# Gated DeltaNet on one core: q projected during the block inversion, q and v parked in SBUF, key norms by products, few subtractions on GpSimd

## The chip, the cores and the metric

The kernel runs on one core of a Trainium2 chip. It has a matrix engine (TensorE, PE in the profile), three engines for elementwise work (VectorE or DVE, ScalarE or ACT, GpSimd or POOL), a queue that issues most transfers (SyncE, SP), a working memory of 128 partitions (SBUF) and an accumulator memory of eight banks that TensorE writes (PSUM). The engines run side by side and wait for each other by semaphores; each takes its instructions in a fixed order. The metric is the device time of one execution in microseconds.

## The reference

A trunk of four layers on 256 frames of 1024 features, in float32. The mixers are gated DeltaNet (GDN, layers 0 and 3), mLSTM (layer 1) and differential attention (layer 2); each is followed by an MLP of width 4096, and each of these eight sub-layers is wrapped in RMS norms. Only GDN and the order of some accumulations change. GDN in short:

```python
proj = h @ w_in                                   # q, k, v, z, gates
qkv = silu(causal_conv(proj[..., :GDN_QKV], conv_w))   # 4 taps in time
q, k, v = l2_norm(q), l2_norm(k), v
kb = kc * bc[..., None]                           # beta * k
a_mat = where(strict, einsum('nbhid,nbhjd->nbhij', kb, kc) * decay, 0)
t_mat = a_mat + eye
sol = triangular_solve(t_mat, concat([vc * beta, kb * exp(gc)]))
attn = einsum('nbhid,nbhjd->nbhij', qc, kc) * decay
# over chunks: v_new = value - kcd @ S;  o = q_inter @ S + attn @ v_new
#              S = S * exp(g_last) + k_state^T @ v_new
return (rms_norm(o, norm_g) * silu(z)) @ w_out
```

## The kernel before

**Products in three parts.** Each weight piece of 128x1024 arrives by one DMA as `raw_*`. `load_w` (L141) copies it on ACT to a short format (`whi_*`, L160), and DVE, or GpSimd for the pieces listed in `pool`, subtracts that copy from the raw piece (`wlo_*`, L166). Activations are split likewise (`hThi`, `hTlo`; `aThi`, `aTlo`). A product is the sum of hi·hi, lo·hi and hi·lo, three matmuls for each step of the contraction. There are four `raw` buffers (NRAW) and eight each of hi and lo (NW); a ninth piece waits until TensorE has finished with one before.

**GDN, in the order of the program** (L943 to L1442). The chunks of the reference are taken as two blocks of 128 frames for each of eight heads; `hg` is a group of four heads, `t` a block of frames.

1. The keys are projected with frames on partitions (`k_block`, tile `gkt`), transposed (`k_channels`, tile `gp`) and convolved in time (`conv`: the first tap on ACT, L1032, three more on DVE, L1038, then silu, L1039). `gates` computes decay and beta in many small steps on DVE; TensorE needs their result `gv` (L1010) for the running sums `gc` (L1016).
2. `decays` broadcasts rows of sums (`gcb`) and makes `Eup` (ACT Abs L1074, then Exp L1079), of which GpSimd keeps the triangles (L1080, L1081).
3. `grams` makes k·k (`gG`). The squared norms of the keys are its diagonal, summed on DVE (L1096, `ssk`); with `c2` = beta over squared norm, `L` becomes the scaled strict triangle (L1105); its 32x32 diagonal blocks are copied to `Lc` by DVE (L1109).
4. `base_inverse` (L1113) inverts all 32x32 blocks at once on DVE: one transpose to `LT` (L1117), 31 steps of a product into `Xt` (L1127) and a subtraction from `Xb` (L1131), 118 small instructions, each step needing the one before, and two transposes to `Xc` and `Yc` (L1132, L1133). `Xb` starts from an identity loaded by DMA (L1353).
5. `levels` joins blocks to 64 and 128 on TensorE, each level with copies on ACT between (`Za`, `Zb`, `zs`, `Ya`, `Yb`, `Zc`, `Yc`, L1136 to L1179); `v_tokens` turns v and scales it with `c1` into `rhs`; `solve`, `state`, `update`, `attend`, `q_norm`, `inter` and `output` follow. `q_norm` gets the squared norms of q by products of squares with a column of ones (`square_sums`, L1056, tile `gss`).
6. The output projection (`finish_mixer`, `out_steps`, tile `acc_wo_g`).

**What sets TensorE's order.** In GDN its order is the program's (`manual`). The projections that nothing waits for yet are generators in the list `blocks`; `fill(us)` takes matmuls off the head of the list until their planned cost (columns / 2400 us for each) is used up, and `finish(key)` takes them until a block is done. The amounts are the table `FILL`, one row for layer 0 and one for layer 3. The other engines' order comes from a scheduler at build time, by program order and readiness; `tc.issue_after(ins)` queues an instruction behind `ins` on the same engine, and the list `hold` does so for the weight splits.

Before, the list holds k and v ahead of the inversion. The blocks of q and z (`conv_block(0, q)`, `z_block`) are appended behind it in the program, and the fill of 23.2 (layer 0) or 21.4 (layer 3) at F[7] comes before the first level. Outputs of the v blocks stay in the PSUM bank, two of them in accumulator banks (`core`), until their convolution reads them.

**MLP and output projections.** Where 512 columns accumulate in each of two halves (`down` L530, `out_steps` L353), a piece of two contraction steps is used in the order k, then half, then the three parts:

```python
for k in range(2):
    for n, hs in enumerate(HALVES):
        seq = [(aTs[j][a][:, 2*q+k, ...], wt(b, k)[:, hs]) for a, b in ((0, 0), (1, 0), (0, 1))]
```

The token projections (`tok_seq`, tiles `mmt`, `gz`, `gkt`) take hi·hi for two k, lo·hi for two k and hi·lo for two k, in one bank.

Of the kernel before, what the change touches and what calls it, by code (L numbers as in the profile page):

```python
# [66 lines left out]
def trunk_kernel(  # L67
# [403 lines left out]
    def mlp(li, hT, first, second):  # L471
# [58 lines left out]
        def down(t, j, q):  # L530
            if (j, q) not in w2t:
                r0 = j * 512 + q * 256
                w2t[j, q] = load_w(w2[r0 : r0 + 256, :].rearrange("(k p) c -> p k c", p=P), 2, D, f"w2_{li}_{j}_{q}")
# [3 lines left out]
            for k in range(2):
                for n, hs in enumerate(HALVES):
                    seq = [(aTs[j][a][:, 2 * q + k, t * P : (t + 1) * P], wt(b, k)[:, hs]) for a, b in ((0, 0), (1, 0), (0, 1))]
                    tail = 3 if t and 8 * (j - nb + 2) + 4 * q + 2 * k + n >= TAIL[0] else 0  # L540
                    run(accs[t][n], seq, start=(j, q, k) == (0, 0, 0), stop=(j, q, k) == (nb - 1, 1, 1), tail=tail)
# [401 lines left out]
    def gdn(li, j, hT, first, second):  # L943
# [83 lines left out]
        def conv(s, q, ps, dst):  # L1027

            y = cvt(f"cy_{li}_{s}{q}") if dst is None else dst
# [3 lines left out]
            for ct in range(2):  # L1033
                b = s * 8 + q * 2 + ct
                x = ps[:, ct * T : (ct + 1) * T]
                for d in (1, 2, 3):
# [1 line left out]
                    nc.vector.scalar_tensor_tensor(y[:, ct, d:], x[:, : T - d], cw[:, c : c + 1], y[:, ct, d:], op0=ALU.mult, op1=ALU.add)  # L1038
            nc.scalar.activation(y, y, AF.Silu)  # L1039
            if s == 0:  # L1040
                squares[q] = cvt(f"csq_{li}_{q}")
                nc.scalar.activation(squares[q], y, AF.Square)
            return y
# [22 lines left out]
        def decays(hg, pr):  # L1066
# [9 lines left out]
            if pr == 1:  # L1076
                for t in range(NT):
                    e = Eup[hg, t]
                    nc.scalar.activation(e, e, AF.Exp, scale=-1.0)  # L1079
# [4 lines left out]
        def grams(hg):

            cols = slice(4 * hg, 4 * hg + 4)
            G = {}
# [10 lines left out]
            nc.vector.tensor_scalar(th8(ssk)[:, :, cols], th8(ssk)[:, :, cols], EPS, None, op0=ALU.add)
            nc.vector.reciprocal(th8(rk2)[:, :, cols], th8(ssk)[:, :, cols])
            nc.vector.tensor_tensor(th8(c2)[:, :, cols], th8(rk2)[:, :, cols], th8(beta)[:, :, cols], op=ALU.mult)  # L1100
            for t in range(NT):
                for h in range(4):
# [2 lines left out]
                    nc.vector.scalar_tensor_tensor(lo, G[t][:, h * P : (h + 1) * P], c2[:, c : c + 1], lo, op0=ALU.mult, op1=ALU.mult)  # L1105
# [32 lines left out]
        def levels():  # L1138
# [9 lines left out]
            nc.scalar.activation(zs[Q[2]], zb[Q[2]], AF.Copy, scale=-1.0)  # L1148
            for b in range(NB):
                for hg in range(2):  # L1150
                    nc.scalar.activation(yts[hg][Q[b], :, Q[b]], Yc[Q[b], hg * 8 : hg * 8 + 8, :], AF.Copy)
# [351 lines left out]
```

## Time and profile before

| quantity | value |
|---|---|
| median of 3 runs | 1379.69 us (1378.94 to 1380.14) |
| the profiled execution | 1379.3 us |
| its span, first to last instruction | 1377.6 us |
| mean granted TensorE clock | 0.974 |
| TensorE matmul, busy | 1308.7 us (95%), 8010 instructions |
| VectorE, busy | 850.9 us (62%), 1493 instructions |
| ScalarE, busy | 725.0 us (53%), 1226 instructions |
| GpSimd, busy | 244.6 us (18%), 225 instructions |
| moved by DMA | 222.77 MB, mean 162 GB/s |

Times in the profile count from the span's start. Layer 0's GDN runs from there to about 204 us, layer 3's from about 1000 to 1187 us; between lie MLP, mLSTM, MLP, attention and MLP. An engine's busy time includes time in which an instruction that has been issued is held up, so a long duration of a small instruction can be a wait. Matmuls overlap; the step from one start to the next tells their rate. A row of a group reads: line, engine, operation, output<-inputs, shapes, count | busy us, mean ns | idle time before them and what ended it. A row of the wait list reads: who waited <- for what: total us, times, longest. A row of the timeline or the chain starts with its start and its length in us.

### The profile page before, as it was taken

To read this page: it belongs to the slowest core of one execution; us is meant where nothing else is said; L and a number is where in the kernel's file an instruction comes from. 1 tells how busy PE (TensorE), PEld (TensorE's weight loads), DVE (VectorE), ACT (ScalarE), POOL (GpSimd) and SP (SyncE) were. 2 spreads that over 40 slices of the span, in tenths; PEclk is the share of its full clock that TensorE was granted. 3 is DMA by queue.
4 is the path that set the end of the run, shared out by engine and by line. 5 is a ranking of instruction groups with operands and counts; after the bars stand their busy time and mean duration, and the time that the engine had idled before them with its cause. 6 is when DMAs were issued, how large, how long until landed. Compare 5 with 4: busy or idle time off the path is not lost.

```text
span 1377.6 us, 20856 instructions
## 1 busy us (share of the span) xinstructions
PE 1308.7 (95%) x8010; PEld 1135.3 (82%) x8010; DVE 850.9 (62%) x1493; ACT 725.0 (53%) x1226; POOL 244.6 (18%) x225
## 2 busy tenths in 40 slices
PE   8885999999999999999999999999999499999998
PEld 5784978898888888989877788989879488899996
DVE  5696577555575786555555477555577944865452
ACT  6754756444454555444465656444467285555441
POOL 2492340000010110000031110000047427000000
PEclk9897999999999999999998999999999799999999
DMA  7452148565655356665463147555554413566650
GB/s 255 130 164 82 47 139 259 184 183 184 201 179 173 99 183 213 191 185 190 138 212 123 62 156 241 184 184 185 185 165 118 123 63 123 167 203 190 183 190 33
DMA packets 131627, 222.77 MB, mean 162 GB/s; under 512 B 10883, under 2 KB 81093, under 8 KB 131526
## 3 DMA queue, kind: packets, MB, share of 16 engines
q1 hardware_dynamic: 131524, 221.42, 50.7%
q8 instruction: 63, 1.03, 0.3%
q14 instruction: 38, 0.31, 0.1%
q10 hardware_dynamic: 2, 0.00, 0.0%
HBM read 220.35 MB, written 1.05 MB: 161 GB/s over the span
## 4 chain that ended last, share of the span: by engine, by line
PE 81%; DVE 11%; ACT 3%; DMA 2%; issue 1%; POOL 1%; SPq 0%; DVEq 0%; POOLq 0%; ACTq 0%
PE acc_mlp L174 26%; PE mmc L174 20%; PE mmt L174 6%; PE acc_wo_g L174 3%; PE gz L174 3%; DVE Xb L1131 2%; DVE Xt L1127 2%; PE dq L174 2%; PE dv L174 2%; PE mo L174 2%; PE acc_wo_d L174 2%; PE acc_wo_m L174 2%; PE mqk L174 2%; PE gp L174 2%; PE acc_S L174 2%
## 5 line engine op out<-in xcount | busy, mean ns | idle before, releaser
L166 DVE TENSOR_TENSOR wlo_w<-raw_w,whi_w 128x1024 fp32r<-128x1024 f32 x256 | 307.2, 1223 | 217.4 <-ACT whi_w L160 216.8
L160 ACT ACTIVATE whi_w<-raw_w 128x1024 fp32r<-128x1024 f32 x256 | 264.3, 1056 | 220.2 <-PE mmc L174 103.3
L174 PE MATMUL acc_mlp<-whi_w,aThi 128*128 128x512 f32 x512 | 202.9, 396 | 0.0
L174 PE MATMUL acc_mlp<-whi_w,aTlo 128*128 128x512 f32 x512 | 202.5, 396 | 0.0
L174 PE MATMUL acc_mlp<-wlo_w,aThi 128*128 128x512 f32 x512 | 202.5, 395 | 0.0
L139 POOL TENSOR_TENSOR rr<-ms,mhalf 128x1 f32<-128x1 f32 x32 | 17.4, 544 | 604.7 <-DVE ms L251 604.7
L174 PEld LDWEIGHTS acc_mlp<-wlo_w,aThi 128*128 128x128 f32 x512 | 96.3, 188 | 23.3
L174 PEld LDWEIGHTS acc_mlp<-whi_w,aThi 128*128 128x128 f32 x512 | 96.4, 188 | 22.0
L174 PEld LDWEIGHTS acc_mlp<-whi_w,aTlo 128*128 128x128 f32 x512 | 96.3, 188 | 22.0
L174 PE MATMUL mmc<-hThi,wlo_w 128*128 128x256 f32 x768 | 108.7, 283 | 0.0
L174 PE MATMUL mmc<-hTlo,whi_w 128*128 128x256 f32 x768 | 107.8, 283 | 0.0
L174 PE MATMUL mmc<-hThi,whi_w 128*128 128x256 f32 x768 | 107.7, 283 | 0.0
L174 PEld LDWEIGHTS mmc<-hThi,whi_w 128*128 128x128 f32 x768 | 99.9, 191 | 1.8
L174 PEld LDWEIGHTS mmc<-hThi,wlo_w 128*128 128x128 f32 x768 | 99.3, 192 | 0.0
L174 PEld LDWEIGHTS mmc<-hTlo,whi_w 128*128 128x128 f32 x768 | 99.0, 192 | 0.0
L166 POOL TENSOR_TENSOR wlo_g<-raw_g,whi_g 128x1024 fp32r<-128x1024 f32 x32 | 76.0, 2406 | 33.5 <-ACT whi_g L160 29.1
L524 ACT ACTIVATE aThi<-rc 128x512 fp32r<-128x512 f32 x48 | 30.3, 632 | 77.8 <-DVE rc L522 77.8
L525 DVE TENSOR_TENSOR aTlo<-rc,aThi 128x512 fp32r<-128x512 f32 x48 | 33.2, 692 | 32.6 <-ACT aThi L524 32.6
L166 POOL TENSOR_TENSOR wlo_wo_g<-raw_wo_g,whi_wo_g 128x1024 fp32r<-128x1024 f32 x16 | 37.6, 2376 | 45.5 <-ACT whi_wo_g L160 44.5
L166 POOL TENSOR_TENSOR wlo_gz<-raw_gz,whi_gz 128x1024 fp32r<-128x1024 f32 x16 | 37.7, 2391 | 42.9 <-ACT whi_gz L160 42.9
L225 ACT ACTIVATE hThi<-T_pre 128x512 fp32r<-128x512 f32 x32 | 17.5, 595 | 49.9 <-PE T_pre L220 49.9
L160 ACT ACTIVATE whi_g<-raw_g 128x1024 fp32r<-128x1024 f32 x32 | 33.3, 1059 | 15.4 <-DMA raw_g<-in_gdn_w_in_dram 11.6
(418 smaller groups left out, 2566.5 us busy)
## 6 DMA issues: line engine op xcount, KB each, us to landing
raw_w<-in_mlp_w_dram SPq DMA_DIRECT2D x256, 512.0 KB, 4.2
raw_g<-in_gdn_w_in_dram SPq DMA_DIRECT2D x32, 512.0 KB, 3.8
raw_gk<-in_gdn_w_in_dram SPq DMA_DIRECT2D x16, 512.0 KB, 5.0
raw_gz<-in_gdn_w_in_dram SPq DMA_DIRECT2D x16, 512.0 KB, 3.6
raw_wo_g<-in_gdn_w_out_dram SPq DMA_DIRECT2D x16, 512.0 KB, 3.3
raw_d<-in_diff_w_in_dram SPq DMA_DIRECT2D x16, 512.0 KB, 4.4
gpost<-in_norm_g_dram SPq DMA_DIRECT2D x8, 512.0 KB, 4.8
raw_mv<-in_mlstm_w_in_dram SPq DMA_DIRECT2D x8, 512.0 KB, 4.5
```

What stands on the lines that cost most here:

```text
L139: return nc.gpsimd.tensor_tensor(dst, src, m, op=ALU.pow)
L160: nc.scalar.activation(hi, raw, AF.Copy)
L166: eng.tensor_tensor(lo, raw, hi.bitcast(F32), op=ALU.subtract)
L174: nc.tensor.matmul(o, l, r, start=start, stop=stop)
L225: a = nc.scalar.activation(hs, ps3, AF.Copy)
L524: nc.scalar.activation(hs, r, AF.Copy)
L525: nc.vector.tensor_tensor(aTs[j][1][:, 2 * q : 2 * q + 2, :].rearrange("p a b -> p (a b)"), r, hs.bitcast(F32), op=ALU.subtract)
L1127: nc.vector.tensor_tensor(t3, LT[:, c : c + 1, rs].to_broadcast([P, m, r1 - r0]), Xb[:, :m, c : c + 1].to_broadcast([P, m, r1 - r0]), op=A ...
L1131: nc.vector.tensor_tensor(Xb[:, :m, rs], Xb[:, :m, rs], t3, op=ALU.subtract)
```

## The change

Parts, in the order of the program:

- Accumulations: half first, then the six products of a piece (hi·hi for both k, lo·hi for both, hi·lo for both) in two runs of three.
- Subtractions on GpSimd: of GDN's weights only those of v2 and v3 stay there (4 a layer); those of v0, v1, q, z and the output weights go to DVE.
- The list `blocks` holds v0 to v3 and then q0 to q3 from the start; each block's output is copied by ACT to SBUF (`gin`, in buffers of `nrm` for v and `cvt` for q). q's weights are requested before the grams.
- `conv` is split into `taps` and `silu`. The keys' four silus and squares are queued on ACT behind the last Exp of `decays`.
- `k_norm` takes the keys' squared norms by `square_sums` ahead of each `grams`; the diagonal sums go. `Lc` is copied by ACT. The reciprocal roots `rk` and `c1` are made once for all 16 columns, behind `base_inverse` in the program.
- Memsets of `Y` and `X` move ahead of the end of k1.
- v's convolutions are behind the inversion on DVE, q's behind `finish("q3")`; z joins the list after v's; z's weights are requested earlier than z's first matmul.
- In `levels` ten copies are queued behind the two `zs` copies.
- `FILL` has new amounts; F[26] and F[27] now stand behind each group's second `decays`.

```diff
-Z_POOL = (0, 1)
+Z_POOL = ()
+GZ_POOL = ()
+GP_POOL = {0: ((),) * 4, 2: ((), (), (0, 1), (0, 1))}
 FILL = (
-    (0.7, 0.7, 0.2, 2.7, 1.1, 1, 3.6, 23.2, 0, 2.7, 6.1, 1.4, 2, 0, 1.6, 0, 1, 0.6, 0.5, 0.6, 2.4, 1.6, 0, 0.1, 0, 4.3, 0, 1.9, 0.2, 1.8, 0.8, 0, 0.1),
-    (0.6, 0.6, 0, 2.2, 1.2, 1, 3.4, 21.4, 0, 3, 5.9, 1.9, 2, 0, 0.4, 0, 1.2, 1.4, 1.4, 0.7, 2.3, 1.3, 0.2, 0, 0, 3.5, 0, 2, 0, 1.8, 2.5, 0, 1),
+    (0.7, 0.7, 0, 5.1, 0.9, 1.2, 3.6, 14, 0, 2.7, 6.1, 0.2, 2, 0, 1.6, 0, 0, 1.8, 1.7, 0.6, 1.2, 1.6, 0, 0.1, 0, 4.3, 0, 3.3, 0.2, 10, 0.8, 0, 0.1),
+    (0.6, 0.6, 0, 2.2, 1.2, 0, 3.4, 14, 0, 4.2, 5.4, 1.9, 2, 0, 0.4, 0, 1.2, 1.4, 1.4, 0.2, 3.3, 0.8, 0.2, 0.3, 0, 3.5, 0.5, 2.5, 0, 10, 2.5, 0, 1),
 )
...
-            for k in range(2):
-                for n, q in enumerate(HALVES):
-                    seq = [(oT[a][:, 2 * i + k, :], chunk(i)(b, k)[:, q]) for a, b in ((0, 0), (1, 0), (0, 1))]
...
+            for n, q in enumerate(HALVES):
+                seq = [(oT[a][:, 2 * i + k, :], chunk(i)(b, k)[:, q]) for a, b in ((0, 0), (1, 0), (0, 1)) for k in range(2)]
+                for m in range(2):
+                    late = tail is not None and 4 * i + 2 * n + m >= TAIL[0]
+                    run(acc[n], seq[3 * m : 3 * m + 3], i == 0 and m == 0, i == 3 and m == 1, 3 if late else 0, tail)
...
-            conv_in[s, q] = ps
-            if s == 0 and alloc is bank:
-                conv_in[s, q] = mid(f"gq_{li}_{q}")
-                nc.scalar.activation(conv_in[s, q], ps, AF.Copy)
+            conv_in[s, q] = (nrm if s else lambda name: cvt(name).rearrange("p a t -> p (a t)"))(f"gin_{li}_{s}{q}")
+            nc.scalar.activation(conv_in[s, q], ps, AF.Copy)
...
+        def silu(s, q, y):
             nc.scalar.activation(y, y, AF.Silu)
-            if s == 0:
-                squares[q] = cvt(f"csq_{li}_{q}")
+            if s < 2:
+                squares[q] = cvt(f"csq_{li}_{s}{q}")
+                return nc.scalar.activation(squares[q], y, AF.Square).ins
...
+        def k_norm(hg):
+            cols = slice(4 * hg, 4 * hg + 4)
+            square_sums(hg, th8(ssk)[:, :, cols])
+            nc.vector.reciprocal(th8(rk2)[:, :, cols], th8(ssk)[:, :, cols])
+            nc.vector.tensor_tensor(th8(c2)[:, :, cols], th8(rk2)[:, :, cols], th8(beta)[:, :, cols], op=ALU.mult)
...
-                    nc.vector.scalar_tensor_tensor(junk, G[t][:, h * P : (h + 1) * P], 1.0, ident, op0=ALU.mult, op1=ALU.mult,
-                                                   accum_out=ssk[:, c : c + 1])
...
-                nc.vector.tensor_copy(Lc[bs, hg * 8 : hg * 8 + 8, :], src)
-            rsqrt(th8(rk)[:, :, cols], th8(ssk)[:, :, cols])
-            nc.vector.tensor_tensor(th8(c1)[:, :, cols], th8(rk)[:, :, cols], th8(beta)[:, :, cols], op=ALU.mult)
+                nc.scalar.activation(Lc[bs, hg * 8 : hg * 8 + 8, :], src, AF.Copy)
...
+            z = nc.scalar.activation(zs[Q[2]], zb[Q[2]], AF.Copy, scale=-1.0).ins
+            with tc.issue_after(z):
...
-            blocks.extend((f"v{q}", conv_block(2, q, bank if q < 2 else lambda name, q=q: core(q - 2, name))) for q in range(4))
+            blocks.extend((f"{'q v'[s]}{q}", conv_block(s, q)) for s in (2, 0) for q in range(4))
...
-            hold.append(sel)
+            hold.extend(ends)
+            end = ends[1]
+            for hg in range(2):
+                with tc.issue_after(end):
+                    for q in (2 * hg, 2 * hg + 1):
+                        end = silu(1, q, k_half(q))
+            hold.append(end)
+            for q in range(4):
+                conv_weights(0, q)
...
+                k_norm(hg)
+                grams(hg)
+                fill(F[5 + hg])
...
             base_end = base_inverse()
             hold.append(base_end)
+            rsqrt(rk, ssk)
+            nc.vector.tensor_tensor(c1, rk, beta, op=ALU.mult)
...
+            fill(F[7])
+            for hg in range(2):
+                k_tokens(hg)
+            finish("v3")
             with tc.issue_after(base_end):
+                convs(2)
+            fill(F[29])
+            with tc.issue_after(base_end):
                 blocks.extend((f"z{t}{hg}", z_block(hg, t)) for t in range(NT) for hg in range(2))
+                z_weights(0)
                 lv = levels()
                 next(lv)
...
+                fill(F[8])
                 next(lv)
+                fill(F[9])
+                for i in range(4):
+                    next(lv)
+                    fill(F[10 + i])
+                    if i < 2:
+                        v_tokens(i)
+                        fill(F[14 + i])
+                solve(0, 0)
...
+                finish("q3")
+                convs(0)
```

(`convs(s)` runs `taps` and `silu` for the four blocks of v or q; `down` of the MLP changes as `out_steps` does.)

More of the change, by code (lines that the diff above doesn't have):

```diff
@@ L536, in down @@
                 accs[t] = new_acc(t, f"mlp{li}")
[L537 to L541, printed above, removed]
+            for n, hs in enumerate(HALVES):
+                seq = [(aTs[j][a][:, 2 * q + k, t * P : (t + 1) * P], wt(b, k)[:, hs]) for a, b in ((0, 0), (1, 0), (0, 1)) for k in range(2)]
+                for m in range(2):
+                    tail = 3 if t and 8 * (j - nb + 2) + 4 * q + 2 * n + m >= TAIL[0] else 0
+                    run(accs[t][n], seq[3 * m : 3 * m + 3], start=(j, q, m) == (0, 0, 0), stop=(j, q, m) == (nb - 1, 1, 1), tail=tail)
         for j in range(2, nb):
@@ L1191, in v_tokens @@
         def v_tokens(q):
+            turned.add(q)
             pv = tbank(f"gv_{li}_{q}")
@@ L1316, in gdn @@
             fill(F[1])
-            for q in range(2):
-                k_channels(q)
             kT = [four(f"gkT{hg}_{li}") for hg in range(2)]
@@ L1321, in gdn @@
             for q in range(2):
-                conv(1, q, conv_in[1, q], k_half(q))
+                k_channels(q)
+            for q in range(2):
+                taps(1, q, conv_in[1, q], k_half(q))
             fill(F[2])
@@ L1346, in gdn @@
                     with tc.high_priority():
-                        sel = decays(hg, pr)
-                    fill(F[26 + 2 * hg + pr])
-            hold.append(sel)
+                        ends = decays(hg, pr)
+                    fill(F[26 + hg] if pr else 0)
+            hold.extend(ends)
+            end = ends[1]
+            for hg in range(2):
+                with tc.issue_after(end):
[4 more added lines that the diff above has]
+                conv_weights(0, q)
             Lc = mid(f"Lc_{li}").rearrange("p (n c) -> p n c", c=BASE)
@@ L1374, in gdn, with convs @@
             qT = [four(f"gqT{hg}_{li}") for hg in range(2)]
-            rhs = {(t, hg): nrm(f"grhs{t}{hg}_{li}").rearrange("p (h d) -> p h d", d=P) for hg in range(2) for t in range(NT)}
+            def convs(s):
+                for q in range(4):
+                    if s == 2:
+                        y = vc[q] = zg[q // 2][:, HALVES[q % 2]].rearrange("p (a t) -> p a t", t=T)
+                    else:
+                        y = qT[q // 2][:, 2 * (q % 2) : 2 * (q % 2) + 2, :]
+                    taps(s, q, conv_in[s, q], y)
+                    silu(s, q, y)
@@ L1382, in gdn @@
[L1382 to L1387 removed]
+                z_weights(0)
                 lv = levels()
                 next(lv)
[L1390 removed]
+                rhs = {(t, hg): nrm(f"grhs{t}{hg}_{li}").rearrange("p (h d) -> p h d", d=P) for hg in range(2) for t in range(NT)}
+                fill(F[8])
```

98 lines of the change are left out of this document (27 added, 71 removed).

## The prediction

> **What bounds the kernel now.** First the page's 40 slices and its span, then what TensorE waited for.
>
> ```profile
> span 1377.6 us, 20856 instructions
> PE   8885999999999999999999999999999499999998
> PEclk9897999999999999999998999999999799999999
> PE Za L1136 <- DVE Yc L1133: 38.2, 2, 19.7
> PE gc L174 <- DVE gv L1010: 8.1, 2, 5.4
> PE T_wo_g L220 <- DVE zg L1268: 4.1, 2, 2.5
> ```
>
> TensorE (PE) is busy nearly everywhere; the digits 5 and 4 are one slice in each of the two GDN layers (0 and 3), and the clock falls there too. The wait list says why: 38.2 us in two waits for `Yc`, the last tile of the block inversion on VectorE (DVE). So outside GDN a saved microsecond must be TensorE work, and inside it a saved wait counts. Next, layer 0's timeline around the inversion, then its instructions grouped by shape.
>
> ```profile
> 83.82 2.13 DVE L1117 STREAM_TRANSPOSE LT<-Lc 128x1024 f32<-128x1024 f32 x1
> 84.16 9.51 POOL L166 TENSOR_TENSOR wlo_g<-raw_g,whi_g 128x1024 fp32r<-128x1024 f32 x4
> 93.63 9.36 POOL L166 TENSOR_TENSOR wlo_gz<-raw_gz,whi_gz 128x1024 fp32r<-128x1024 f32 x4
> 102.94 0.28 DVE L1127 TENSOR_TENSOR Xt<-LT,Xb 128x28 f32<-128x28 f32 x2
> 117.50 1.05 DVE L1132 STREAM_TRANSPOSE Xc<-Xb 128x512 f32<-128x512 f32 x1
> 118.58 0.71 DVE L1133 STREAM_TRANSPOSE Yc<-Xc 128x512 f32<-128x512 f32 x1
> L1131 DVE TENSOR_TENSOR Xb<-Xb,Xt 128x15 f32<-128x15 f32 x6 | 14.3, 2413 | 0.0
> L1131 DVE TENSOR_TENSOR Xb<-Xb,Xt 128x28 f32<-128x28 f32 x12 | 1.9, 190 | 0.0
> 100.90:119.40 18.50, 0.05 (x1) 0.00 (x0) 18.26 (x115) 0.82 (x2) 2.09 (x1) 0.57 0.20 63
> ```
>
> From 83.8 to 119.3 the inversion takes 35.5 us. While GpSimd (POOL) subtracts, a step of 15 columns takes 2413 ns; afterwards one of 28 columns takes 190. From 102.94 to 117.50 the rest runs in 14.6 us. With the first eight instructions at that pace (0.8), LT 2.1 and the two closing transposes 1.8, the chain alone is **19.3 us**; 16.2 are waits for GpSimd. The last row is the window view (length, then busy time and count of PE, weight loads, DVE, ACT, POOL, and the clock): from 100.9 on TensorE has no placed work left, and ScalarE (ACT) none either.
>
> **The change, part by part.** The sum is against the profiled execution, 1379.3 us (span 1377.6); the median of the runs is 1379.69.
>
> *1. Gates (−9.2).* 56 of 64 subtractions leave GpSimd.
>
> ```profile
> L166 POOL TENSOR_TENSOR wlo_g<-raw_g,whi_g 128x1024 fp32r<-128x1024 f32 x32 | 76.0, 2406 | 33.5 <-ACT whi_g L160 29.1 <-PE gkt L174 4.4
> L166 DVE TENSOR_TENSOR wlo_gk<-raw_gk,whi_gk 128x1024 fp32r<-128x1024 f32 x16 | 19.3, 1224 | 9.9 <-ACT whi_gk L160 9.8
> L1003 DVE TENSOR_TENSOR gyv<-gcc,dtb 128x16 f32<-128x16 f32 x2 | 4.3, 2167 | 0.1
> 36.60:42.00 5.40, 0.04 (x1) 0.00 (x0) 4.94 (x13) 2.51 (x5) 3.02 (x2) 0.70 0.51 181
> 42.00:50.00 8.00, 7.99 (x24) 6.27 (x25) 4.60 (x14) 3.14 (x7) 3.72 (x2) 0.57 0.57 170
> 43.88 1.05 PE L174 MATMUL gkt<-whi_gk,hTlo 128*128 128x512 f32 x2
> 47.29 1.05 PE L174 MATMUL gkt<-wlo_gk,hThi 128*128 128x512 f32 x2
> ```
>
> The gate chain's small operations wait for GpSimd as the inversion's do (`gyv`: 2167 ns for 16 columns), and TensorE waits 8.1 us for their end. Halves of v0 and v1 move to DVE at 1224 ns, so the chain meets at most a 1.2 us instruction: I keep 1.5 us of the wait. In layer 0 the 5.4 us of idleness are followed by a clock of 0.57: from 43.88 to 47.29 eight matmuls take 3.41, 0.196 each over the 0.23 of the full clock, and thirteen run so: 2.6 us. −8.1 − 2.6 + 1.5.
>
> *2. q beside the inversion (−41.2).*
>
> ```profile
> 252.02 11.50 PE mmc L174 x96
> 93.92 1.04 PE L1186 MATMUL gkd<-csq,gkT 128*128 128x128 f32 x8
> 80.36 2.16 DVE L1105 SCALAR_TENSOR_TENSOR L<-gG,gc,L 128x128 f32<-128x128 f32 x8
> L1151 ACT ACTIVATE Y<-Yc 32x256 f32<-32x256 f32 x16 | 5.8, 406 | 0.1
> L139 POOL TENSOR_TENSOR hrr<-hss,mhalf 128x4 f32<-128x4 f32 x12 | 12.1, 1011 | 29.8 <-DVE hss L236 28.2 <-DVE hrr L239 1.5
> L139 POOL TENSOR_TENSOR grk<-gck,mhalf 128x8 f32<-128x8 f32 x4 | 6.6, 1656 | 0.8 <-DVE gck L1098 0.8
> 1101.20:1106.00 4.80, 4.80 (x78) 4.74 (x79) 4.80 (x13) 4.70 (x11) 0.00 (x0) 0.50 0.02 5
> ```
>
> The fill from the last gram to the first level is 14 + 10 units of 2.4 GHz time, 26.9 us at the real step (11.50 us for 96 matmuls is 0.120, the fill counts 0.107), plus the two groups of `gkd` 2.1 and the 4.0 of fill before LT: 33 us of TensorE work. DVE from the last gram: half of L's eight 1.1, LT and chain 19.3, six of q's eight subtractions 7.3, and a wait for one `pow` of 16 columns on GpSimd. The pow's row of 8 columns bounds it from below and twice that from above; I take 2.9, going on from 1.01 (4 columns) and 1.66 (8). The four copies of `Lc` become ACT's, 1.6 by the row of `Y`. Together 32.2 against 33: the cover just holds and the 38.2 go, with the half clock behind them (0.50 for 4.8 us in layer 3; I take 1.5 a layer). Were q's weights late, this cover would be gone (rival C). Their loads pass SP's queue behind v's, with the load of `Xb` after them; all eight need v's buffers, and v is done 12 us into the 33. At nothing go the evacuations of v and q and the copies (ACT's idle 17.7 us of the window row hide them; without that cover, some 0.6 each), and the memsets moved ahead (GpSimd has lost four subtractions there).
>
> *3. Norms by products (+6.7).*
>
> ```profile
> 159.95 1.68 PE gss L174 x16
> ```
>
> 16 products with a column of ones took 1.68 us; four such groups are added, on TensorE, which has no slack there. The 32 diagonal sums leave DVE, but its chain isn't late there any more.
>
> *4. A wait ahead of them (+15.8).*
>
> ```profile
> 52.53 0.73 PE L174 MATMUL gcb<-rows_g,ident 40*128 40x256 f32 x4
> 55.22 3.21 ACT L1074 ACTIVATE Eup<-gcb,ngc 128x128 f32<-128x128 f32 x12
> 58.45 1.28 ACT L1079 ACT_TABLE_LOAD   x1
> L1042 ACT ACTIVATE csq<-gqT 128x512 f32<-128x512 f32 x8 | 4.8, 630 | 0.0
> ```
>
> The first products now need the keys' squares, and the keys' silu is placed behind the last decay exponential on ACT. From the first `gcb`: about 1 to start, 16 Abs at 0.27 = 4.3, table 1.28, four Exp at 0.58 = 2.3, table 1.28, two silus and two squares 2.5: 12.7 us. TensorE has `gcb` with its waits (3.7) and 3.3 units of fill (3.7): idle 5.3. After such an idleness part 1 lost 2.6. I take 5.4 + 2.5 a layer; bounds 0 (ACT does the silus earlier than I add up) and 12 (as much other ACT work slips in between). Queued behind the waiting product are the grams and so the inversion, whose cover I count from the grams on.
>
> *5. Behind the inversion (+7).*
>
> ```profile
> 119.22 7.07 DVE L1038 SCALAR_TENSOR_TENSOR cy<-gp,cw,cy 128x255 f32<-128x255 f32 x18
> 125.20 0.57 ACT L1147 ACTIVATE zs<-Za 32x512 f32<-32x512 f32 x1
> 125.79 0.59 ACT L1148 ACTIVATE zs<-Zb 32x512 f32<-32x512 f32 x1
> ```
>
> Between the first two levels no fill is left, so TensorE waits for two copies on ACT (0.57 and 0.59) and their hand-over, some 1.5 us; before the third it has 3 to 4.7 us of fill against 15 copies (6 us): 3.5 a layer. Bounds 0 and 12. DVE gets v's and q's taps (24 at 7.07/18 = 0.39, 9.4 us a set) and eight subtractions of z and of the output weights (9.8 each) there: 38 us of the some 60 that TensorE works; z's first one ends about 11 us behind the inversion, TensorE asks at 14.
>
> *6. Output norms (−3).*
>
> ```profile
> 172.66 2.09 DVE L239 TENSOR_TENSOR hrr<-hrr,grq 128x4 f32<-128x4 f32 x1
> 204.66 9.17 PE mmt L174 x40
> 240.81 11.20 PE acc_mlp L174 x48
> ```
>
> `hrr` waits 2.09 us for GpSimd's output subtractions, and TensorE 4.1 in all for what follows; a DVE subtraction in the way costs 1.2 at most.
>
> *7. Order of the accumulations (−4).* 1536 + 384 matmuls keep operands and loads; six instead of three go to one half in a row, hi before lo. `mmt`, ordered like that, takes 229.2 ns a step, `acc_mlp` 233.3. The price lies between 0 and 4.1 × 1920 = −7.9; I see no cause in the rows and take the middle. [...]
>
> −9.2 − 41.2 + 6.7 + 15.8 + 7 − 3 − 4 = −27.9: **1351.4 us**.
>
> **Rivals.**
> - A: the fills cover parts 4 and 5 (ACT faster than I add up; that it stands idle in the window row shows room, but later; against it, its table loads and Abs can't shrink): 22.8 less, 1328.6.
> - B: both waits twice as long, near their upper bounds (the sums of ACT times leave out what slips in between): 1374.2.
> - C: q doesn't run beside the inversion, its halves arriving late: 10 us a layer stay idle, 1371. Against it: DVE is free while ACT makes the squares.
> - D: the order of the accumulations doesn't matter, `acc_mlp` stays at 233.3 ns: part 7 is 0, 1355.4. For it: operands and loads stay the same.
> - E, slower: ACT's order behind the inversion. Before, the two copies after `Za` started at 125.20, 5.9 us behind `Yc` (118.58 + 0.71), other copies and conversions ahead of them, and 6.1 units of fill hid it; that fill is gone. If at five hand-overs (levels to first solve) half of that, 3 us, stands ahead, TensorE loses 15 a layer: 1381. Against it: ten of those copies are now ordered behind the two. It decides from 14 us a layer, half of 27.9.
>
> **How the numbers follow.** Chances: forecast 0.39, A 0.20, D 0.15, B 0.12, C 0.08, E 0.06. The forecast's own range is 1340 to 1363 (A's and B's shares in part). For 8 in 10 the range reaches down past A (part 7 at its full price) and up to B: 1326 to 1374; outside are A with everything favourable and most of E. Less than 0.2% (2.8 us) can't be told from no change: A, D, the forecast and seven eighths of C are faster, B is split 0.07, 0.03, 0.02, E mostly slower: 0.89, 0.05, 0.06.
>
> **What would show it.** Right: no wait of `Za` for `Yc` over 2 us, step instructions near 0.2 us throughout, `gp` matmuls beside them, the wait for `gv` under 2 us, 64 more `gss`, a new wait of `gss` for ACT's squares of about 5 us a layer, small ones at `Ya` and `Zc`. A step of `acc_mlp` near 229 or 233 settles part 7. Wrong: `Za` still waiting over 5 us, steps of over 1 us in the inversion beyond one pow a layer, or TensorE waiting for z's low halves.

## The result, and the profile after

The changed kernel took **1357.3 us** (median of 4 runs, 1354.9 to 1361.3), the kernel before, beside it, 1379.9: ratio 0.984, interval 0.981 to 0.987. That is 22.6 us, between 18 and 26, where 27.9 had been forecast. Six more runs gave 1356.9 and the same ratio (`c_after` below). The profiled execution is the slowest of the four, 1361.3 us with a span of 1359.5; the traces differ by 18.1 us.

First the page of the changed kernel (span, busy time of the engines, slices), then what TensorE waited for.

```profile
span 1359.5 us, 20901 instructions
PE 1323.8 (97%) x8074; PEld 1151.0 (85%) x8074; DVE 840.6 (62%) x1467; ACT 727.0 (53%) x1254; POOL 111.9 (8%) x167
PE   7899999999999999999999999999998999999998
PEclk9899999999999999999999999999997999999999
```

```profile
PE gss L176 <- ACT csq L1048: 4.8, 2, 3.6
PE gc L176 <- DVE gv L1014: 3.8, 2, 3.1
PE gkt L176 <- DVE grow_g L461: 2.5, 1, 2.5
PE T_wo_g L222 <- DVE zg L1270: 1.9, 1, 1.9
PE acc_wo_g L176 <- ACT oThi_wo_g L230: 1.6, 2, 0.8
PE Zc L176 <- ACT Y L1165: 1.5, 1, 1.5
PE Ya L1136 <- ACT zs L1147: 1.3, 2, 0.7
PE Yb L1136 <- ACT zs L1148: 0.7, 2, 0.4
```

The 38.2 us of `Za` waiting for `Yc` are gone from the list, and the digits 5 and 4 from the slices. GpSimd's busy time fell from 244.6 us to 111.9. But the clock still shows an 8 in layer 0 and a 7 in layer 3.

**Where the time went.** The window view, over the two GDN layers and over layer 2's attention (length, then busy time and count of PE, weight loads, DVE, ACT, POOL, the clock, the DMA share, GB/s), before:

```profile
0.00:215.00 215.00, 180.92 (x1271) 157.50 (x1272) 148.03 (x385) 128.38 (x264) 97.51 (x69) 0.93 0.45 141
690.00:800.00 110.00, 108.58 (x502) 82.11 (x502) 59.23 (x109) 64.08 (x156) 26.61 (x57) 0.92 0.39 131
985.00:1200.00 215.00, 188.95 (x1346) 166.90 (x1345) 147.97 (x394) 127.23 (x265) 97.56 (x59) 0.95 0.40 124
```

and after:

```profile
0.00:215.00 215.00, 197.98 (x1345) 172.39 (x1346) 149.24 (x380) 137.21 (x286) 31.12 (x40) 0.94 0.47 153
690.00:800.00 110.00, 108.54 (x517) 83.14 (x517) 61.25 (x118) 64.01 (x159) 23.45 (x52) 0.97 0.40 135
985.00:1200.00 215.00, 205.12 (x1432) 182.38 (x1431) 153.09 (x385) 139.20 (x284) 27.74 (x25) 0.95 0.43 136
```

Length less busy time is TensorE's idle time: 34.1 to 17.0 us in layer 0, 26.1 to 9.9 in layer 3, 33.3 us won. The clock hardly rose although long idle stretches went away that mostly show a clock of 0.5 (0.50 from 104 to 119 us and from 1087 to 1101 before), so busy time at half clock must have grown. The same view in steps of 1 us gives it (busy time times what the clock lacks to 1, summed):

| busy time lost to the half clock, us | before | after | `c_after` |
|---|---|---|---|
| layer 0 (0 to 215) | 5.8 | 11.3 | 7.8 |
| attention (690 to 800) | 8.5 | 3.4 | 3.4 |
| layer 3 (985 to 1200) | 2.9 | 9.5 | 10.2 |

So 33.3 us of idleness were won, and 12.1 us came back as matmuls at half clock in the two GDN layers, and some 6.5 as the 64 new products. The 5.1 us of the attention have nothing to do with the change: with the same attention, other traces show 8.5 (`e1`, `e5`) or 1.7 (`e3`). −33.3 + 12.1 + 6.5 − 5.1 is −19.8 against −18.1 measured. The 1.7 us that are missing are on the page: TensorE's busy time rose by 15.1 us (1308.7 to 1323.8), which is 7.0 of half clock, 6.5 of products and 1.6 of other work that these rows do not place.

### The profile page after: what moved, and what is told of

Same layout as the page of the kernel before. It is cut to its first block, busy times and chain, and to the rows that moved or that the text cites. A ratio compares the mean times of both kernels' runs of the same rounds, so it can differ in the third digit from the quotient of the medians.

```text
span 1359.5 us, 20901 instructions
## 1 busy us (share of the span) xinstructions
PE 1323.8 (97%) x8074; PEld 1151.0 (85%) x8074; DVE 840.6 (62%) x1467; ACT 727.0 (53%) x1254; POOL 111.9 (8%) x167
## 4 chain that ended last, share of the span: by engine, by line
PE 87%; ACT 4%; DVE 3%; DMA 3%; issue 1%; POOL 1%; SPq 0%; DVEq 0%; POOLq 0%; ACTq 0%
PE acc_mlp L176 26%; PE mmc L176 20%; PE mmt L176 6%; PE gp L176 6%; PE gz L176 3%; PE acc_wo_g L176 2%; PE dq L176 2%; PE dv L176 2%; PE mo L176 2%; PE acc_wo_d L176 2%; PE acc_wo_m L176 2%; PE mqk L176 2%; PE gkt L176 2%; PE acc_S L176 1%; PE gss L176 1%
## 5 line engine op out<-in xcount | busy, mean ns | idle before, releaser
L168 DVE TENSOR_TENSOR wlo_w<-raw_w,whi_w 128x1024 fp32r<-128x1024 f32 x256 | 302.9, 1221 | 224.5 <-ACT whi_w L162 223.8
L162 ACT ACTIVATE whi_w<-raw_w 128x1024 fp32r<-128x1024 f32 x256 | 258.8, 1052 | 227.0 <-issue 136.8
L176 PE MATMUL acc_mlp<-whi_w,aTlo 128*128 128x512 f32 x512 | 161.7, 396 | 0.0
L176 PE MATMUL acc_mlp<-whi_w,aThi 128*128 128x512 f32 x512 | 161.1, 396 | 0.0
L176 PE MATMUL acc_mlp<-wlo_w,aThi 128*128 128x512 f32 x512 | 161.0, 395 | 0.0
L141 POOL TENSOR_TENSOR rr<-ms,mhalf 128x1 f32<-128x1 f32 x32 | 17.5, 548 | 547.0 <-DVE ms L253 547.0
L176 PE MATMUL mmt<-whi_w,hTlo 128*128 128x512 f32 x128 | 40.2, 395 | 0.0
L176 PE MATMUL mmt<-whi_w,hThi 128*128 128x512 f32 x128 | 40.1, 394 | 0.0
L176 PE MATMUL mmt<-wlo_w,hThi 128*128 128x512 f32 x128 | 40.1, 394 | 0.0
```

The source lines that it names most:

```text
L141: return nc.gpsimd.tensor_tensor(dst, src, m, op=ALU.pow)
L162: nc.scalar.activation(hi, raw, AF.Copy)
L168: eng.tensor_tensor(lo, raw, hi.bitcast(F32), op=ALU.subtract)
L176: nc.tensor.matmul(o, l, r, start=start, stop=stop)
```

## The experiments

Medians, with the ratio to the kernel before, which ran beside each of them. That kernel gave medians of 1378.0 to 1379.6 there, and single runs from 1373.6 to 1383.4.

| run | us | ratio, interval |
|---|---|---|
| `c_after`: the changed kernel | 1356.9 | 0.984 (0.981 to 0.986) |
| `e1_old_order` | 1360.3 | 0.986 (0.982 to 0.990) |
| `e2_fill_ahead` | 1360.1 | 0.986 (0.984 to 0.989) |
| `e3_gates_first` | 1356.5 | 0.984 (0.981 to 0.987) |
| `e4_silu_free` | 1357.2 | 0.985 (0.982 to 0.988) |
| `e5_diagonal_norms` | 1351.8 | 0.981 (0.977 to 0.984) |
| `e6_q_on_gpsimd` | 1379.9 | 1.002 (1.000 to 1.003) |
| `e7_before_vector` | 1378.3 | 1.000 (0.998 to 1.002) |
| `e8_less_cover` | 1378.8 | 0.999 (0.998 to 1.001) |
| `e9_diagonal_silu_free` | 1356.5 | 0.983 (0.981 to 0.985) |
| `e10_diagonal_more_cover` | 1353.0 | 0.980 (0.978 to 0.982) |
| `e12_diagonal_gates` | 1348.5 | 0.978 (0.976 to 0.980) |

**The scatter.** `c_after` is the changed kernel without an edit.

> The changed kernel itself, to see its own scatter. Its four runs so far lie between 1354.9 and 1361.3 us, while those of the kernel before lie within 2 us. Theory: the scatter is the clock. Span times granted clock is nearly constant in them (1359.5 x 0.980 = 1332, 1357.9 x 0.982 = 1333, 1353.4 x 0.985 = 1333), so longer runs should again show a lower clock and the product should stay within 1330 to 1336. Rival: the scatter is in waits or transfers, then the product varies with the time by several us.

Six runs, 1351.6 to 1360.3 us, with mean clocks from 0.987 (the fastest) to 0.980. Span times clock lies between 1331.7 and 1332.8 in five of them and at 1328.9 in one. So the scatter is mostly the clock's, as expected (the bound was missed once, by 1.1). Small edits must therefore be read in the trace, since a median of four to six runs moves by 3 us by itself. A trace is one execution, too: those of `e2`, `e6`, `e10` and `e12` are the fastest of their runs, those of `e5` and `e9` the slowest.

**Is q beside the inversion enough, or GpSimd's absence?** Three runs. First the kernel before with one part alone:

```diff
-Z_POOL = (0, 1)
+Z_POOL = ()
...
-                zck[hg] = tok_chunks(w, 3 * hk + hg * 512, f"gz{li}_{hg}", (0, 1, 2, 3))
+                zck[hg] = tok_chunks(w, 3 * hk + hg * 512, f"gz{li}_{hg}", ())
...
-            wts[s, q] = load_w(w_cols(w, s * hk + q * 256, 256), KT, 256, f"g{li}_{s}{q}", (0, 1))
+            wts[s, q] = load_w(w_cols(w, s * hk + q * 256, 256), KT, 256, f"g{li}_{s}{q}", (0, 1) if s == 2 and q > 1 else ())
```

> The kernel before with one part of the change alone: the subtractions of v0, v1, q, z and the output weights on DVE in place of GpSimd. Theory: the gates' wait of 8.1 us shrinks to about 3, and the inversion of 35.5 us loses its 16.2 us of waits for GpSimd but takes in those of the eight subtractions of q and z that come in it, 9.8 us at most; TensorE still runs out of placed work at about 100 us in layer 0, so Za waits 8 to 14 us a layer instead of 19: 1379 - 5 - 14 = 1360, between 1354 and 1368. Rival: without q beside the inversion nothing is won there, Za still waits 17 us or more a layer, 1374.

Nothing was won (1378.3): a miss, and 4 us above even the rival, whose reason (`Za` waiting for `Yc`) did not come either. Its wait list:

```profile
PE gp L174 <- DVE wlo_g L166: 35.7, 2, 18.6
```

DVE's timeline in layer 0:

```profile
83.72 2.04 DVE L1117 STREAM_TRANSPOSE LT<-Lc 128x1024 f32<-128x1024 f32 x1
102.20 0.71 DVE L1133 STREAM_TRANSPOSE Yc<-Xc 128x512 f32<-128x512 f32 x1
102.84 4.59 DVE L166 TENSOR_TENSOR wlo_g<-raw_g,whi_g 128x1024 fp32r<-128x1024 f32 x4
```

and TensorE's, with the wait in brackets:

```profile
104.08 2.36 PE L174 MATMUL gp<-hThi,wlo_g 128*128 128x256 f32 x8 [18.57 <-DVE wlo_g L166]
```

The inversion now takes 19.2 us from `LT` to the end of `Yc` (35.5 before): with GpSimd quiet its own length is what the prediction had worked out, 19.3. But the kernel before requests q's weights under `issue_after(base_end)`, so on DVE their subtractions queue behind the inversion, and TensorE waits for them as long as it had waited for the inversion. 38.2 us became 35.7 under another name.

Second, the changed kernel with q's subtractions back on GpSimd:

```diff
-GP_POOL = {0: ((),) * 4, 2: ((), (), (0, 1), (0, 1))}
+GP_POOL = {0: ((0, 1),) * 4, 2: ((), (), (0, 1), (0, 1))}
```

> The subtractions of q's weights, which now lie beside the inversion, go back to GpSimd; the order of the work is the changed one. Theory: both halves of part 2 are needed. While GpSimd subtracts (2.4 us each, eight a layer), the small instructions of the inversion are held; the chain grows from 26.9 us by 19 less the 7.3 that DVE no longer spends, to some 36 to 38, against a cover of about 29 from LT on: Za waits 7 to 9 us a layer for Yc, with half clock behind it, 1357 + 18 = 1375. Rival: placing q beside the inversion is all that counts and the engine of its subtractions is not: no wait of Za over 2 us, 1357 to 1360.

All of the gain is gone. The wait list:

```profile
PE Za L1136 <- DVE Yc L1133: 8.8, 2, 6.0
PE Ya L1136 <- ACT zs L1147: 6.8, 2, 6.1
```

The inversion's first and last tile in layer 0, and its steps of 15 columns in the view grouped by shape, of this kernel:

```profile
76.33 2.14 DVE L1117 STREAM_TRANSPOSE LT<-Lc 128x1024 f32<-128x1024 f32 x1 [1.82 <-ACT Lc L1111]
107.23 0.71 DVE L1133 STREAM_TRANSPOSE Yc<-Xc 128x512 f32<-128x512 f32 x1
L1131 DVE TENSOR_TENSOR Xb<-Xb,Xt 128x15 f32<-128x15 f32 x6 | 5.2, 896 | 0.0
```

and of the changed one, followed by its timelines of DVE and TensorE in layer 0:

```profile
L1131 DVE TENSOR_TENSOR Xb<-Xb,Xt 128x15 f32<-128x15 f32 x6 | 1.0, 173 | 0.0
```

```profile
79.67 2.12 DVE L1117 STREAM_TRANSPOSE LT<-Lc 128x1024 f32<-128x1024 f32 x1 [1.74 <-ACT Lc L1111]
105.84 0.71 DVE L1133 STREAM_TRANSPOSE Yc<-Xc 128x512 f32<-128x512 f32 x1
```

```profile
108.44 0.21 PE L1136 MATMUL Za<-Yc,L 32*32 32x32 f32 x1
```

Beside GpSimd a step takes 896 ns on the mean, without it 173. The direction was as expected; the time came out 5 us above the 1375, and the waits are not the expected ones: the chain grew from 26.9 us to 31.6, not to 36 or more, `Za` waits 2.8 and 6.0 us, and ACT's copies behind it come late in layer 3 (6.1). The rows leave open which of the two carries how much of the 23 us.

Third, the dose: less fill beside the inversion.

```diff
-    (0.7, 0.7, 0, 5.1, 0.9, 1.2, 3.6, 14, 0, 2.7, 6.1, 0.2, 2, 0, 1.6, 0, 0, 1.8, 1.7, 0.6, 1.2, 1.6, 0, 0.1, 0, 4.3, 0, 3.3, 0.2, 10, 0.8, 0, 0.1),
-    (0.6, 0.6, 0, 2.2, 1.2, 0, 3.4, 14, 0, 4.2, 5.4, 1.9, 2, 0, 0.4, 0, 1.2, 1.4, 1.4, 0.2, 3.3, 0.8, 0.2, 0.3, 0, 3.5, 0.5, 2.5, 0, 10, 2.5, 0, 1),
+    (0.7, 0.7, 0, 5.1, 0.9, 1.2, 3.6, 14, 0, 2.7, 6.1, 0.2, 2, 0, 1.6, 0, 0, 1.8, 1.7, 0.6, 1.2, 1.6, 0, 0.1, 0, 4.3, 0, 3.3, 0.2, 0, 0.8, 0, 0.1),
+    (0.6, 0.6, 0, 2.2, 1.2, 0, 3.4, 14, 0, 4.2, 5.4, 1.9, 2, 0, 0.4, 0, 1.2, 1.4, 1.4, 0.2, 3.3, 0.8, 0.2, 0.3, 0, 3.5, 0.5, 2.5, 0, 0, 2.5, 0, 1),
```

> The changed kernel with the fill of 10 units between v's end and the first level set to 0 in both layers: some 11 us of q's matmuls a layer come later, between the levels and ahead of q's convolutions, in place of beside the inversion. Theory (part 2): every microsecond of matmuls taken away there is one of waiting; the inversion still ends at about 106.5 us in layer 0, TensorE asks 11 us earlier, Za waits 9 us in layer 0 and 10 to 11 in layer 3, half clock behind each, and the fill that comes later finds little to cover (the waits of Ya and Zc, 3 us): 1357 + 18 = 1375, within 4. Rival: the matmuls set free cover as much later, and the time ends below 1366.

```profile
PE Za L1136 <- DVE Yc L1133: 19.9, 2, 10.5
```

The rows of layer 0 show 9.4 us, those of layer 3 10.5: 19.9 us of waits for some 22 us of matmuls that now come later, and 21.8 us more time. What was moved covers little where it goes (`T_wo_g` and `acc_wo_g` wait 2.2 us less). Together the three say that part 2 takes **both** halves, matmuls to run beside the inversion and a DVE that is neither held by GpSimd nor has q's low halves queued behind the inversion. The second half taken out of the changed kernel, or ten units of the first, cost 23.0 and 21.8 us, all of the gain. The second half alone, in the kernel before, won nothing; the first alone was not run, for `e6` also carries the price of the other parts.

**The order of the accumulations.**

```diff
-            for n, hs in enumerate(HALVES):
-                seq = [(aTs[j][a][:, 2 * q + k, t * P : (t + 1) * P], wt(b, k)[:, hs]) for a, b in ((0, 0), (1, 0), (0, 1)) for k in range(2)]
...
+            for k in range(2):
+                for n, hs in enumerate(HALVES):
+                    seq = [(aTs[j][a][:, 2 * q + k, t * P : (t + 1) * P], wt(b, k)[:, hs]) for a, b in ((0, 0), (1, 0), (0, 1))]
```

> The changed kernel with the accumulations of the MLP and the output projection in the old order (k, then half). Theory: the order is worth nothing, since the step of acc_mlp is 233.3 ns in both traces: the time stays at 1357, within 2 us, and the step at 233.3. Rival (the prediction's part 7): the new order was worth 4 us, so 1361.

The chain that ended last, in the changed kernel and in this one:

```profile
232.22 11.20 PE acc_mlp L176 x48
```

```profile
229.34 11.20 PE acc_mlp L176 x48
```

233.3 ns a step in both orders, and in the kernel before. The median lies 3.4 us higher, but its six runs reach from 1351.3 (faster than any of the changed kernel) to 1368.0, the three longest with clocks of 0.976 and 0.977 against 0.989. TensorE's busy time over the whole trace, less what the half clock took, is 1299.6 us here and 1299.5 and 1300.3 in the two traces of the changed kernel, which leaves no room for 4 us. The order is worth nothing; this is rival D. Why the 512-column step is 233.3 ns in `acc_mlp` and 229.2 in `mmt` stays open.

**The gates.** What keeps `gc` waiting in layer 0? The DVE's timeline of the changed kernel:

```profile
37.55 0.18 DVE L434 SCALAR_TENSOR_TENSOR lp_p<-lp_p,lp_s 128x16 f32<-128x16 f32 x1
40.42 0.48 DVE L1041 SCALAR_TENSOR_TENSOR gkT<-gp,cw,gkT 128x255 f32<-128x255 f32 x1 [2.70 <-ACT gkT L1035]
40.82 0.16 DVE L435 TENSOR_SCALAR lp_p<-lp_p 128x16 f32<-128x16 f32 x1
41.42 1.25 DVE L1041 SCALAR_TENSOR_TENSOR gkT<-gp,cw,gkT 128x255 f32<-128x255 f32 x3
42.59 0.16 DVE L1014 TENSOR_TENSOR gv<-gv,nA 128x16 f32<-128x16 f32 x1
```

and of the kernel before:

```profile
41.78 0.18 DVE L1010 TENSOR_TENSOR gv<-gv,nA 128x16 f32<-128x16 f32 x1
```

`gv` now ends 0.8 us later than before. No small step is held any more (0.16 to 0.18 us each), but the build's order has put taps of the keys ahead of the last three steps, and the DVE sits 2.70 us waiting for their first tap on ACT.

```diff
-            for q in range(4):
-                conv_weights(2, q)
...
-                next(chain)
+                gv_end = next(chain)
+            for q in range(4):
+                conv_weights(2, q, gv_end)
...
-                taps(1, q, conv_in[1, q], k_half(q))
+                with tc.issue_after(gv_end):
+                    taps(1, q, conv_in[1, q], k_half(q))
```

> On DVE the subtractions of v0 and v1 and the taps of the first two key blocks are queued behind the last instruction of the gate chain (gv). Theory: in layer 0 the chain is now late because of DVE's own queue (three subtractions of 1.2 us and four taps ahead of gv), no longer because of GpSimd: gv ends at about 36 us in place of 42.7, gc's wait of 3.1 us goes, and with it the half clock from 44.3 to 48.5 (2.2 us): 1357 - 5 = 1352. Rival: the chain is late by ACT's copies between its steps, gv still ends behind 40 us, and the time stays.

`gv` started at 35.93 and `gc`'s wait left the list; layer 0 ended at 189.1 us (195.8 and 192.9 in the traces of the changed kernel). But layer 3, where `gv` had hardly been late (0.7 us), took 3 us longer in this trace, and the time stayed. Whether the order did that is not shown: the half clock took 12.8 us of layer 3 here against 9.5 and 10.2, and `e1`, without this order, lost the same 12.8. The mechanism in layer 0 was right, the forecast for the whole kernel missed.

**The wait ahead of the norms.** More fill there:

```diff
-    (0.7, 0.7, 0, 5.1, 0.9, 1.2, 3.6, 14, 0, 2.7, 6.1, 0.2, 2, 0, 1.6, 0, 0, 1.8, 1.7, 0.6, 1.2, 1.6, 0, 0.1, 0, 4.3, 0, 3.3, 0.2, 10, 0.8, 0, 0.1),
-    (0.6, 0.6, 0, 2.2, 1.2, 0, 3.4, 14, 0, 4.2, 5.4, 1.9, 2, 0, 0.4, 0, 1.2, 1.4, 1.4, 0.2, 3.3, 0.8, 0.2, 0.3, 0, 3.5, 0.5, 2.5, 0, 10, 2.5, 0, 1),
+    (0.7, 0.7, 0, 5.1, 0.9, 1.2, 3.6, 14, 0, 2.7, 3.1, 0.2, 2, 0, 4.6, 0, 0, 1.8, 1.7, 0.6, 1.2, 1.6, 0, 0.1, 0, 4.3, 0, 6.3, 0.2, 10, 0.8, 0, 0.1),
+    (0.6, 0.6, 0, 2.2, 1.2, 0, 3.4, 14, 0, 4.2, 2, 1.9, 2, 0, 4.2, 0, 1.2, 1.4, 1.4, 0.2, 3.3, 0.8, 0.2, 0.3, 0, 3.5, 0.5, 6.5, 0, 10, 2.5, 0, 1),
```

> 3 (layer 0) and 4 (layer 3) more units of fill ahead of the keys' norms, taken from the fill behind the second level, and as much added behind the first v_tokens. Theory: the wait of gss for the keys' squares (1.2 and 3.6 us) and the half clock behind it (some 14 us at half speed in layer 0, 15 in layer 3) cost 5 and 10 us; with TensorE busy there, gss waits under 1 us and the clock stays at 1.00: 1357 - 12 = 1345. Rival: what is saved there is waited for later, because the DVE is late behind the inversion: the gss wait goes, new waits of the same size come at v_tokens, solve or T_wo_g, and the time stays at 1357.

The wait for the squares left the list and the half clock behind it too (lost busy time 4.8 and 5.6 us in the layers), but new waits came:

```profile
PE T_wo_g L222 <- DVE zg L1270: 6.1, 3, 4.2
PE gv L1198 <- ACT zg L1045: 3.7, 2, 2.0
```

This trace is of the fastest of the six runs (span 1352.6), and there they give back only a part of what was won; the median did not fall all the same (1360.1), and the time is the rival's. The new waits say that fill is a stock: what is spent ahead of the norms is missing at v's turning and at the output norms.

The other way is to have the squares earlier, with the keys' silus free of the order behind the decays:

```diff
-                with tc.issue_after(end):
-                    for q in (2 * hg, 2 * hg + 1):
-                        end = silu(1, q, k_half(q))
...
                 taps(1, q, conv_in[1, q], k_half(q))
+                silu(1, q, k_half(q))
```

> The keys' silus and squares are no longer queued behind the last Exp of the decays: each stands right behind its taps in the program, and the scheduler of the build places it (two of the four land ahead of the decays on ACT, with table loads of 1.28 us between). Theory (the prediction's part 4): the wait of the first gss for the keys' squares comes from that order, so the wait goes (3.3 to 4.8 us in two traces) and part of the half clock behind it: 1357 - 6 = 1351, with the waits of TensorE for gcb and Eup longer by no more than 2 us. Rival: the added table loads delay Eup and the decays by as much, the wait moves to gcb or to the second gss, 1357 or above.

1357.2, no change in the median. `gss` waits 1.8 us instead of 3.3 to 4.8, but `gcb` 5.4 instead of 3.5, and `gp` 3.5 for ACT's copies of the keys, where it hardly waited before: the waits moved, as the rival had it. The half clock did shrink in this trace, to 8.4 us in the two layers against 18.0 and 20.9, while their idle time grew from 25.4 and 26.9 to 30.6. Its span is 1353.8, against 1356.2 and 1359.5, but two of the four runs were 3 to 5 us longer at lower clocks (0.981 and 0.982 against 0.988 and 0.989), so whether something was won stays open.

**The norms.** From the diagonal of k·k on DVE again:

```diff
-            square_sums(hg, th8(ssk)[:, :, cols])
+            nc.vector.tensor_scalar(th8(ssk)[:, :, cols], th8(ssk)[:, :, cols], EPS, None, op0=ALU.add)
...
+                    nc.vector.scalar_tensor_tensor(junk, G[t][:, h * P : (h + 1) * P], 1.0, ident, op0=ALU.mult, op1=ALU.mult,
+                                                   accum_out=ssk[:, c : c + 1])
```

> The keys' squared norms are summed from the diagonal of k.k on DVE again, and the 64 products, their squares on ACT and the wait for them go; everything else as changed. Theory (parts 3 and 4): the products cost TensorE 6.7 us at the full clock, more where they run at half of it, and the diagonal sums (32 of about 0.27 us) put some 4 us a layer on DVE ahead of the inversion, which its cover of 33 us against 32 takes only in part: Za waits 2 to 4 us a layer, and the time ends at 1354, within 4 us. Rival: the products were worth their cost because the inversion has no slack at all: Za waits over 5 us a layer and the time is above 1362.

1351.8, 5 us less than `c_after`; the intervals still overlap a little. `Za` waits 2.1 and 4.3 us, as the theory had it:

```profile
PE Za L1144 <- DVE Yc L1141: 6.3, 2, 4.3
```

TensorE's busy time without the half clock is 1292.6 us, against 1299.5 and 1300.3: this is what the products cost. Next the same with the silus of `e4` (both edits as above):

> Norms from the diagonal and the keys' silus free of the order behind the decays, together. Theory: the two cost the changed kernel in different places (products and their half clock; the idle stretch ahead of them), so the second adds something to the first: TensorE's half-clock loss in the two layers falls below 10 us (14.2 with the diagonal alone) and the time from 1351.8 to 1348. Rival: the silu order alone made no difference to the time (1357.2 against 1356.9), and makes none here: 1350 to 1353, the waits for gcb longer by what the wait ahead of the grams loses.

1356.5, a miss, above even its rival's 1353: `Za` waits 8.5 us there, and the half clock takes 17.5 us in the two layers, not under 10. Why the two edits disturb each other stays open. Then diagonal norms with more cover:

```diff
-    (0.7, 0.7, 0, 5.1, 0.9, 1.2, 3.6, 14, 0, 2.7, 6.1, 0.2, 2, 0, 1.6, 0, 0, 1.8, 1.7, 0.6, 1.2, 1.6, 0, 0.1, 0, 4.3, 0, 3.3, 0.2, 10, 0.8, 0, 0.1),
-    (0.6, 0.6, 0, 2.2, 1.2, 0, 3.4, 14, 0, 4.2, 5.4, 1.9, 2, 0, 0.4, 0, 1.2, 1.4, 1.4, 0.2, 3.3, 0.8, 0.2, 0.3, 0, 3.5, 0.5, 2.5, 0, 10, 2.5, 0, 1),
+    (0.7, 0.7, 0, 5.1, 0.9, 1.2, 3.6, 14, 0, 2.7, 3.6, 0.2, 2, 0, 1.6, 0, 0, 1.8, 1.7, 0.6, 1.2, 1.6, 0, 0.1, 0, 4.3, 0, 3.3, 0.2, 12.5, 0.8, 0, 0.1),
+    (0.6, 0.6, 0, 2.2, 1.2, 0, 3.4, 14, 0, 4.2, 0.9, 1.9, 2, 0, 0.4, 0, 1.2, 1.4, 1.4, 0.2, 3.3, 0.8, 0.2, 0.3, 0, 3.5, 0.5, 2.5, 0, 14.5, 2.5, 0, 1),
```

> Norms from the diagonal, and 2.5 (layer 0) and 4.5 (layer 3) units more fill ahead of the first level, taken from the fill behind the second. Theory: the waits of Za for Yc that the diagonal sums brought (2.1 and 4.3 us) go, with the half clock behind the second one, and half of it comes back at the levels, where as much fill is missing (Zc, gv): 1351.8 - 4 = 1348. Rival: all of it comes back there, 1352 with new waits of Zc or gv of over 4 us.

1353.0: `Za`'s waits are gone, `gv` waits 6.0 us for v's silus instead. The rival, as in `e2`.

**A version faster than both.** Diagonal norms, and the gate order of `e3` in layer 0 alone:

```diff
+                    if not li:
+                        queue.enter_context(tc.issue_after(gv_end))
                     taps(1, q, conv_in[1, q], k_half(q))
```

> Norms from the diagonal, and in layer 0 alone the gate chain ahead of v0's and v1's subtractions and the keys' taps on DVE. Theory: in the trace with the gate chain first in both layers, layer 0 ended at 189.1 us (192.9 and 195.8 in two traces of the changed kernel) while layer 3 took 183.2 us from its first key block to the MLP (180.1 and 180.6 there), so that the gain of one was lost in the other and the time stayed at 1356.5. With layer 3 left as it was, layer 0's gain stays: gc waits under 1 us in layer 0, layer 0 ends by 188 us, and the time is 1351.8 - 4 = 1348. Rival: the front of layer 0 is bound by the whole chain from the gates over the decays to the keys' silus, and what the gates win is waited for at gcb and behind it: 1351 to 1353.

1348.5 us (1346.1 to 1349.6), as expected, and its interval lies wholly below that of the changed kernel. `gc` doesn't wait in layer 0, which ends at 185.5 us (about 192 in `e5`). The interval still overlaps that of `e5`, so what the gates add to the norms rests on the trace.

## Why the prediction came out as it did

The bound and the main term were right, and the forecast was 6 us low (1351.4 against 1357.3). It would have been further off had two misses not cancelled in part: idle time that fell by 3.3 us more than forecast, and half clock that grew. The prediction's terms, sorted by kind, beside the two traces without the attention:

| us | predicted | traces |
|---|---|---|
| TensorE's idle time in GDN (parts 1, 2, 4, 5, 6) | −30.0 | −33.3 |
| half clock in GDN (parts 1, 2, 4) | −0.6 | +12.1 (+9.3 with `c_after`) |
| new products (part 3) | +6.7 | +6.5 |
| order of the accumulations (part 7) | −4 | 0 |

The half clock is the term that was mis-sized: the prediction took 2.6 and 3.0 us away and gave 5.0 back. By its own steps:

- **Gates (−9.2): failed.** "The chain meets at most a 1.2 us instruction" counted GpSimd's hold and forgot the DVE's own queue, where taps came ahead. `gc` still waits 3.8 us (5.2 in `c_after`) of the 8.1, half clock follows it (0.50 to 48.8 us in layer 0), and `gkt`'s 2.5 us wait that ends at 28.5 us in layer 0, 1.5 before, is followed by another stretch of it (0.50 to 35.1) that was not there. So little is left of the term in these traces. In the trace of `e12` an order on DVE won layer 0's part of it.
- **q beside the inversion (−41.2): right**, wait and working. From `LT` to `Yc`'s end 26.9 us were measured, and 26.6 had been worked out (19.3 and six subtractions of 7.3); the `pow` of 16 columns took 2908 ns for 2.9. TensorE asked 1.9 us after `Yc`'s end in layer 0, and 0.7 us after it in layer 3. "The cover just holds" is what `e8` shows from the other side.
- **Products (+6.7)** and **the wait ahead of them (+15.8)**: the wait itself was shorter (4.8 us in all against 10.8), its half clock longer. "I take 2.5 a layer", after the gates' example, was the mis-sized term. The window view in layer 3:

```profile
1028.00:1046.00 18.00, 16.13 (x77) 16.13 (x78) 6.61 (x24) 8.71 (x17) 3.98 (x3) 0.53 0.00 0
```

  and TensorE's timeline there:

```profile
1029.87 3.58 PE L176 MATMUL gss<-ones,csq 128*128 128x1 f32 x16 [3.57 <-ACT csq L1048]
1033.31 3.76 PE L176 MATMUL gG<-gkT 128*128 128x128 f32 x16
1036.86 3.41 PE L176 MATMUL gss<-ones,csq 128*128 128x1 f32 x16
1040.13 3.76 PE L176 MATMUL gG<-gkT 128*128 128x128 f32 x16
1043.55 1.63 PE L176 MATMUL gp<-hThi,wlo_g 128*128 128x256 f32 x6
```

  16 products took 3.4 us from start to start, twice the 1.68 of the prediction, and all four groups ran at half clock: some 7 us lost where 2.5 was taken. In layer 0 it was 5.1 us, and 1.7 of them came ahead of the products, behind two waits for `gcb` of 1.6 and 0.5 us.
- **Behind the inversion (+7)**: 3.5 us of waits (`Ya`, `Yb`, `Zc`). Rival E's queue on ACT did not come in the changed kernel; it did in `e6`.
- **Output norms (−3)**: the wait for `zg` fell from 4.1 to 1.9, but `acc_wo_g` waits 1.6 for ACT: some −0.6.
- **Order of the accumulations (−4)**: 0, rival D.

## What to carry to other kernels

A wait of 38 us had two causes in series, no matmuls to run and a held engine behind them (a step of 15 columns took 2413 ns beside GpSimd, 173 in the changed kernel), and both had to go: with the held engine alone taken away, the wait moved to another name in the wait list, and with it put back the gain was gone. Work to fill gaps with is a stock: before spending it at one wait, ask which later one it covered. And count a wait with the half clock behind it: in layer 3 a wait of 3.6 us was followed by some 7 us lost in products of one column and of 128.
